# The four block sums of the second up projection: transfers that accumulate in place of VectorE

## The chip, the cores and the metric

The kernel runs on one core of a Trainium2 chip. The metric is the time of one execution in microseconds (us) on the device. Five engines take part, each with its own queue worked in order: TensorE (PE in the profile; its weight loads are PEld), VectorE (DVE), ScalarE (ACT), GpSimd (POOL) and SyncE (SP), which here issues all DMA transfers. Sixteen DMA engines carry them out.

## The reference

One layer of a block over 512 tokens of width 1024, in float32: an FFN half step, a mixer of two head groups, and a second FFN half step. The change is in the second FFN:

```python
def _modulate(x, shift, scale):
    return _rms(x) * (1.0 + scale[:, None, :]) + shift[:, None, :]

def _swiglu(h, w_in, w_out):
    gate, up = jnp.split(h @ w_in, 2, axis=-1)
    return (jax.nn.silu(gate) * up) @ w_out

h = _modulate(x, sh3, s3)
x = x + 0.5 * g3[:, None, :] * _swiglu(h, ffn2_w_in[l], ffn2_w_out[l])
```

`ffn2_w_in` is 1024 x 5632: 22 blocks of 128 gate columns and 22 blocks of 128 up columns. `h` has 512 rows.

## The kernel before

Activations lie transposed: 8 tiles of 128 channels x 512 tokens. To keep float32 accuracy every operand of a matmul is split into a high part (a cast to the matmul's type fp32r) and a low part (the rest), and a product is three matmuls: high x high, high x low, low x high. For weights, ScalarE casts the raw block (`wr`) to the high part (`wh`), and VectorE subtracts that from the raw block to get the low part (`wl`).

A **unit** is a block of weights: a load by SyncE into a raw tile of 128 x 1024 (pool tag `wr`, four buffers), and a split into `wh` and `wl` (four buffers each). `plan_units` lists all units in the order of use; `next_unit` takes the next, so loads are written just ahead of use, but SyncE runs ahead as far as raw buffers are free.

The second FFN's up projection (`ffn2`, line 936) computes blocks 0 to 4 and 18 to 21 as plain units. Blocks 5 to 17 (`SEVEN`), 13 of them, are done in pairs: gate block and up block together. `unit_pair` (line 227) loads both, and the gate block `g` and up block `u`, each cut into two halves of 512 input channels, form a 2 x 2 matrix of blocks: a11, a12 from `g` and a21, a22 from `u`. The 512 channels x 256 tokens quarters of the activations form the other 2 x 2 matrix. Their product is made of **seven** block products in place of eight. For that the weights are needed as a11, a12, a22 and as four sums: a21 + a22, that less a11, a11 - a21, and a12 less the second sum. The activations need four differences too, made once by `combined` (line 281) while blocks 2 to 4 run.

`sevenths` (line 234) prepares the weights of a pair in steps. VectorE makes the sums into two tiles of their own (`sf`, two buffers): the first two sums (lines 255 and, through the helper of line 240, `sub`), later the other two (line 240). Three wide splits follow, of `g`, of the first two sums and of the last two (ScalarE at line 244, VectorE at line 240), and a narrow one of a22 (ScalarE at line 274, tiles `sh`, `sl`).

`seven_products` (line 308) runs the seven products of a pair in the order 1, 2, 6, 7, 5, 4, 3, each 12 matmuls at line 323 into PSUM accumulators `za`, `zb`, `zc`. ScalarE and VectorE empty the accumulators between them (lines 327 to 343), since some are continued by later products; line 345 multiplies the SiLU of the gate half by the up half. After each product `side.step()` writes one step of the next pair's `sevenths`, so the weights of a pair are prepared while the pair before it is multiplied. What is left is flushed at the pair's end.

Within an engine the order of instructions is not simply that of the text: the framework's planner takes what has its inputs and buffers ready by its own cost figures, earlier text first. It also inserts all the waits. Some stages fix an order by hand (`in_order`, `matmuls_in_order`); the pairs are not among them.

Of the kernel before, what the change touches and what calls it, by code (L numbers as in the profile page):

```python
# [11 lines left out]
F32 = mybir.dt.float32  # L12
F32R = mybir.dt.float32r
# [3 lines left out]
ALU = mybir.AluOpType  # L17
AX = mybir.AxisListType

P = 128  # L20
# [4 lines left out]
DFF = 2816  # L25
# [16 lines left out]
class Side:  # L42
# [5 lines left out]
    def add(self, *gens):  # L48
        self.todo.extend(gens)
# [40 lines left out]
class Block:  # L90
# [136 lines left out]
    def unit_pair(self, w, c):  # L227

        raws = [self.raw_tile() for _ in range(2)]
        for raw, o in zip(raws, (c, DFF + c)):  # L230
            self.load(raw, w[:, o:o + P].rearrange("(k p) f -> p k f", p=P))
        return lambda: self.sevenths(*raws)

    def sevenths(self, g, u):

        nc = self.nc
        lo4, hi4 = slice(0, 4), slice(4, 8)
        a11, a12, a21, a22 = g[:, lo4], g[:, hi4], u[:, lo4], u[:, hi4]
        new = lambda dt, tag: self.seven.tile([P, 8, P], dt, tag=tag, name=self.name(tag))
        sub = lambda out, x, y: nc.vector.tensor_tensor(out=out, in0=x, in1=y, op=ALU.subtract)  # L240

        def parts(raw, n=8):
            hi, lo = (self.wp.tile([P, 8, P], F32R, tag=t, name=self.name(t)) for t in ("wh", "wl"))
            nc.scalar.copy(hi[:, :n], raw[:, :n])  # L244
            yield hi, lo
            sub(lo[:, :n], raw[:, :n], hi[:, :n].bitcast(F32))
            yield

        def steps():
            out = {}  # L250
            gate = parts(g)
            hi, lo = next(gate)
            out[1], out[2] = (hi[:, lo4], lo[:, lo4]), (hi[:, hi4], lo[:, hi4])
            s12, s34 = new(F32, "sf"), new(F32, "sf")
            nc.vector.tensor_tensor(out=s12[:, lo4], in0=a21, in1=a22, op=ALU.add)
            sub(s12[:, hi4], s12[:, lo4], a11)
            yield
            next(gate)
            p12 = parts(s12)
            hi, lo = next(p12)  # L260
            out[5], out[6] = (hi[:, lo4], lo[:, lo4]), (hi[:, hi4], lo[:, hi4])
            yield
            sub(s34[:, lo4], a11, a21)
            sub(s34[:, hi4], a12, s12[:, hi4])
            yield
            next(p12)
            p34 = parts(s34)
            hi, lo = next(p34)
            out[7], out[3] = (hi[:, lo4], lo[:, lo4]), (hi[:, hi4], lo[:, hi4])
            yield  # L270
            next(p34)
            yield
            hi, lo = (self.seven.tile([P, 4, P], F32R, tag=t, name=self.name(t)) for t in ("sh", "sl"))
            nc.scalar.copy(hi, a22)
            sub(lo, a22, hi.bitcast(F32))
            out[4] = hi, lo
            yield
            self.weights7 = out
        return steps()

    def combined(self):

        nc, v = self.nc, self.nc.vector
        f = lambda x: x.bitcast(F32)
        l, r = slice(0, HALF), slice(HALF, NT)
        sub = lambda out, x, y: v.tensor_tensor(out=out, in0=x, in1=y, op=ALU.subtract)
        self.t7 = {1: [], 2: [], 3: [], 4: []}
        for j in range(4):
            x = []
            for h in (self.h[j], self.h[j + 4]):  # L290
                x.append(self.slot(s="hx"))
                v.tensor_tensor(out=x[-1], in0=f(h[0]), in1=f(h[1]), op=ALU.add)
            yield
            a, b = x
            t12, t34 = self.slot(s="t7"), self.slot(s="t7")
            sub(t12[:, l], a[:, r], a[:, l])
            sub(t12[:, r], b[:, r], t12[:, l])
            yield
            sub(t34[:, l], b[:, r], a[:, r])
            sub(t34[:, r], b[:, l], t12[:, r])  # L300
            yield
            for t, n in ((t12, 1), (t34, 3)):
                hi, lo = self.split(t, "t")
                self.t7[n].append((hi[:, l], lo[:, l]))
                self.t7[n + 1].append((hi[:, r], lo[:, r]))
            yield

    def seven_products(self, w, side):

        nc = self.nc  # L310
        l, r = slice(0, HALF), slice(HALF, NT)
        half = lambda ks, ts: [(self.h[k][0][:, ts], self.h[k][1][:, ts]) for k in ks]
        xs = {1: half(range(4), l), 2: half(range(4, 8), l), 3: half(range(4, 8), r), 4: self.t7[4], 5: self.t7[1],
              6: self.t7[2], 7: self.t7[3]}
        za, zb, zc = self.acc()[:, :HALF], self.aux()[:, :HALF], self.aux()[:, :HALF]
        sa, sb, sg, up = (self.slot(s=n) for n in ("pa", "pb", "sg", "up"))

        def product(z, n, start):
            hi, lo = w[n]
            for j in range(4):  # L320
                xh, xl = xs[n][j]
                for i, (a, b) in enumerate(((hi, xh), (hi, xl), (lo, xh))):
                    nc.tensor.matmul(z, a[:, j, :], b, start=start and j == 0 and i == 0, stop=j == 3 and i == 2,  # L323
                                     skip_group_check=not start)
            side.step()

        add = lambda out, x, y: nc.vector.tensor_tensor(out=out, in0=x, in1=y, op=ALU.add)
        product(za, 1, True)
        nc.scalar.copy(sa[:, l], za)
        product(zc, 2, True)  # L330
        add(sg[:, l], zc, sa[:, l])
        nc.scalar.activation(sg[:, l], sg[:, l], AF.Silu)
        product(za, 6, False)
        nc.scalar.copy(sa[:, r], za)
        product(zb, 7, True)
        nc.scalar.copy(sb[:, l], zb)
        product(za, 5, False)
        nc.scalar.copy(sb[:, r], za)
        product(zb, 4, False)
        add(up[:, r], sb[:, l], sb[:, r])  # L340
        add(up[:, l], zb, sa[:, r])
        product(za, 3, False)
        nc.scalar.activation(sg[:, r], za, AF.Silu)
        a = self.slot(s="af")
        self.mul(a, sg, up)
        return a

    def unit_wide(self, src):
# [1736 lines left out]
```

## Time and profile before

| what | value |
|---|---|
| median of 2 runs | 1064.16 us (1063.7 to 1064.62) |
| profiled execution | 1067.01 us |
| its span, first to last instruction | 1065.3 us |
| mean granted clock of TensorE | 0.994 |
| TensorE busy | 1047.7 us, 98% of the span |
| VectorE busy | 649.5 us, 61% |
| ScalarE busy | 436.8 us, 41% |
| GpSimd busy | 24.9 us, 2% |
| bytes moved by DMA | 130.67 MB |

Times in a trace are counted from the first instruction. A line such as L240 is a line of the kernel; where a helper issues several operations they share its line and are told apart by their tiles (`out<-in`). A group's row gives the count, the total busy time and the mean of one, and then the idle time of the engine just before and what ended it. The releaser of a wait is inferred from the semaphores. The thirteen pairs run from about 760 to 893 us.

### The profile page before, as it was taken

To read this page: it belongs to the slowest core of one execution; us is meant where nothing else is said; L and a number is where in the kernel's file an instruction comes from. 1 tells how busy PE (TensorE), PEld (TensorE's weight loads), DVE (VectorE), ACT (ScalarE), POOL (GpSimd) and SP (SyncE) were. 2 spreads that over 40 slices of the span, in tenths; PEclk is the share of its full clock that TensorE was granted. 3 is DMA by queue.
4 is the path that set the end of the run, shared out by engine and by line. 5 is a ranking of instruction groups with operands and counts; after the bars stand their busy time and mean duration, and the time that the engine had idled before them with its cause. 6 is when DMAs were issued, how large, how long until landed. Compare 5 with 4: busy or idle time off the path is not lost.

```text
span 1065.3 us, 15289 instructions
## 1 busy us (share of the span) xinstructions
PE 1047.7 (98%) x6021; PEld 894.8 (84%) x6021; DVE 649.5 (61%) x1149; ACT 436.8 (41%) x772; POOL 24.9 (2%) x74
## 2 busy tenths in 40 slices
PE   6999999999999999999999989999999999999998
PEld 5788878788887799888788769998899999888887
DVE  4487984333576527557878567877878786532221
ACT  3342322222222215658865554444455555422220
POOL 1000000000000000100000001100000000000000
PEclk8999999999999999999999999999999999999999
DMA  9979973333597324421222021105233433333320
GB/s 276 281 231 302 284 233 98 99 99 94 169 305 248 113 80 141 113 60 40 60 75 70 21 79 41 40 14 146 60 110 94 114 107 112 90 94 109 108 66 30
DMA packets 207766, 130.67 MB, mean 123 GB/s; under 512 B 13633, under 2 KB 191822, under 8 KB 207694
## 3 DMA queue, kind: packets, MB, share of 16 engines
q1 hardware_dynamic: 207694, 129.69, 41.2%
q8 instruction: 47, 0.77, 0.3%
q14 instruction: 25, 0.20, 0.1%
HBM read 127.18 MB, written 2.49 MB: 122 GB/s over the span
## 4 chain that ended last, share of the span: by engine, by line
PE 93%; DVE 3%; issue 1%; DMA 1%; SPq 0%; POOL 0%; ACT 0%; POOLq 0%
PE pa L431 22%; PE pa L433 22%; PE pa L432 22%; PE pa L323 7%; PE pb L323 5%; PE pb L1818 1%; DMA ar<-in_w_ada 1%; PE pb L580 1%; PE pb L432 1%; PE pb L431 1%; PE pb L433 1%; PE pb L1798 1%; PE pb L1418 1%; PE pb L1370 1%; PE pb L1800 0%
## 5 line engine op out<-in xcount | busy, mean ns | idle before, releaser
L205 ACT CAST wh<-wr 128x1024 fp32r<-128x1024 f32 (+1 forms) x138 | 139.6, 1015 | 359.2 <-PE pa L432 272.9
L206 DVE TENSOR_TENSOR wl<-wr,wh 128x1024 fp32r<-128x1024 f32 (+1 forms) x138 | 162.4, 1179 | 173.2 <-ACT wh L205 167.7
L431 PE MATMUL pa<-hh,wh 128*128 128x512 f32 (+1 forms) x629 | 243.6, 387 | 0.0
L433 PE MATMUL pa<-hh,wl 128*128 128x512 f32 (+1 forms) x629 | 241.2, 383 | 0.0
L432 PE MATMUL pa<-hl,wh 128*128 128x512 f32 (+1 forms) x629 | 241.1, 383 | 0.0
L431 PE MATMUL pa<-ah,wh 128*128 128x512 f32 (+1 forms) x396 | 146.3, 370 | 0.0
L433 PE MATMUL pa<-ah,wl 128*128 128x512 f32 (+1 forms) x396 | 144.9, 366 | 0.0
L432 PE MATMUL pa<-al,wh 128*128 128x512 f32 (+1 forms) x396 | 144.8, 366 | 0.0
L431 PEld LDWEIGHTS pa<-hh,wh 128*128 128x128 f32 x629 | 118.3, 188 | 25.4 <-issue 2.9
L433 PEld LDWEIGHTS pa<-hh,wl 128*128 128x128 f32 x629 | 118.3, 188 | 22.9 <-DVE wl L206 0.4
L432 PEld LDWEIGHTS pa<-hl,wh 128*128 128x128 f32 x629 | 118.4, 188 | 21.1 <-DVE hl L617 0.2
L431 PEld LDWEIGHTS pa<-ah,wh 128*128 128x128 f32 x396 | 74.7, 189 | 13.5 <-ACT wh L205 1.7
L433 PEld LDWEIGHTS pa<-ah,wl 128*128 128x128 f32 x396 | 74.7, 189 | 12.2
L432 PEld LDWEIGHTS pa<-al,wh 128*128 128x128 f32 x396 | 74.7, 189 | 11.9
L748 DVE SCALAR_TENSOR_TENSOR aa<-ar,sc,aa 128x512 f32<-128x512 f32 x98 | 73.2, 750 | 11.4 <-DMA ar<-in_w_ada 10.3
L794 DVE TENSOR_TENSOR af<-sg,pa 128x512 f32<-128x512 f32 x27 | 18.5, 686 | 50.3 <-PE pa L433 50.3
L240 DVE TENSOR_TENSOR wl<-sf,wh 128x1024 fp32r<-128x1024 f32 x26 | 31.9, 1225 | 21.0 <-ACT wh L244 20.2
L860 DVE SCALAR_TENSOR_TENSOR xT<-pa,mod,xT 128x512 f32<-128x512 f32 (+1 forms) x18 | 12.4, 692 | 50.9 <-PE pa L433 50.9
L244 ACT CAST wh<-sf 128x1024 fp32r<-128x1024 f32 x26 | 27.2, 1048 | 30.1 <-PE pa L323 12.4
L800 ACT CAST ah<-af 128x512 fp32r<-128x512 f32 x44 | 25.9, 621 | 16.2 <-DVE af L794 16.2
L431 PE MATMUL pa<-mh,wh 128*128 128x256 f32 (+1 forms) x96 | 31.8, 333 | 0.0
L432 PE MATMUL pa<-ml,wh 128*128 128x256 f32 (+1 forms) x96 | 30.9, 322 | 0.3 <-DVE ml L1846 0.3
(434 smaller groups left out, 1811.6 us busy)
## 6 DMA issues: line engine op xcount, KB each, us to landing
wr<-in_ffn_w_in SPq DMA_DIRECT2D x79, 512.0 KB, 4.8
ar<-in_w_ada SPq DMA_DIRECT2D x48, 512.0 KB, 6.2
wr<-in_ffn_w_out SPq DMA_DIRECT2D x32, 512.0 KB, 4.1
ar<-in_w_ada SPq DMA_DIRECT2D x48, 256.0 KB, 5.0
wr<-in_w_in SPq DMA_DIRECT2D x21, 512.0 KB, 3.6
wr<-in_ffn_w_out SPq DMA_DIRECT2D x16, 384.0 KB, 4.4
wr<-in_w_out SPq DMA_DIRECT2D x8, 512.0 KB
wr<-in_ffn_w_in SPq DMA_DIRECT2D x8, 384.0 KB, 7.2
```

Source lines behind the costliest of these rows:

```text
L205: self.nc.scalar.copy(hi, raw)
L206: self.nc.vector.tensor_tensor(out=lo, in0=raw, in1=hi.bitcast(F32), op=ALU.subtract)
L240: sub = lambda out, x, y: nc.vector.tensor_tensor(out=out, in0=x, in1=y, op=ALU.subtract)
L244: nc.scalar.copy(hi[:, :n], raw[:, :n])
L323: nc.tensor.matmul(z, a[:, j, :], b, start=start and j == 0 and i == 0, stop=j == 3 and i == 2, skip_group_check=not start)
L431: mm(out, wh, xh, start=start, stop=False)
L432: mm(out, wh, xl, start=False, stop=False)
L433: mm(out, wl, xh, start=False, stop=stop)
L748: nc.vector.scalar_tensor_tensor(out=acc, in0=a, scalar=sc, in1=acc, op0=ALU.mult, op1=ALU.add)
L794: nc.vector.tensor_tensor(out=a, in0=s, in1=pu, op=ALU.mult)
L800: nc.scalar.copy(ah, a)
L860: nc.vector.scalar_tensor_tensor(out=self.xT[t][:, ts], in0=p[:, ts], scalar=gate[:, t:t + 1], in1=self.xT[t][:, ts], op0=ALU.mult, op1=AL ...
```

## The change

The pair's loads get a third one: a22 once more, into a tile `s2` of its own (two buffers). `sevenths` no longer has tiles `sf`. The four sums are made by DMA transfers that add to what is at their destination (`accum_op=ALU.add`), issued by GpSimd, and they overwrite the raw tiles:

- g low half += u low half (a11 + a21),
- u low half += u high half (a21 + a22),
- s2 += g low half (a22 + a11 + a21),
- g high half += s2 (a12 + a22 + a11 + a21).

A transfer of this kind can only add, so the signs differ from before: the up block counts as negated. The differences in `combined` change signs accordingly, by a `scalar_tensor_tensor` with a factor of -1 in half of them, and line 345 multiplies by -1.

Since `g` is overwritten, its split comes first, and all four transfers are written in the step after it. Then `u` (now a21 + a22, and a22) is split in one wide split, `s2` in the narrow one, and `g` a second time in the last wide split. So there are three wide splits and one narrow one, as before.

```diff
-        return lambda: self.sevenths(*raws)
+        s2 = self.seven.tile([P, 4, P], F32, tag="s2", name=self.name("s2"))
+        self.load(s2, w[4 * P:, DFF + c:DFF + c + P].rearrange("(k p) f -> p k f", p=P))
+        return lambda: self.sevenths(*raws, s2)
...
+        plus = lambda out, x: nc.gpsimd.dma_start(out=out, in_=x, accum_op=ALU.add)
+
+        def parts(raw):
+            n = raw.shape[1]
+            pool, tags = (self.wp, ("wh", "wl")) if n == 8 else (self.seven, ("sh", "sl"))
+            hi, lo = (pool.tile([P, n, P], F32R, tag=t, name=self.name(t)) for t in tags)
+            nc.scalar.copy(hi, raw)
             yield hi, lo
+            nc.vector.tensor_tensor(out=lo, in0=raw, in1=hi.bitcast(F32), op=ALU.subtract)
             yield
+
+        def both(p):
+            hi, lo = p
+            return [(hi[:, x], lo[:, x]) for x in (lo4, hi4)]
 
         def steps():
             out = {}
-            gate = parts(g)
-            hi, lo = next(gate)
-            out[1], out[2] = (hi[:, lo4], lo[:, lo4]), (hi[:, hi4], lo[:, hi4])
-            s12, s34 = new(F32, "sf"), new(F32, "sf")
-            nc.vector.tensor_tensor(out=s12[:, lo4], in0=a21, in1=a22, op=ALU.add)
-            sub(s12[:, hi4], s12[:, lo4], a11)
-            yield
-            next(gate)
-            p12 = parts(s12)
...
-            sub(s34[:, lo4], a11, a21)
-            sub(s34[:, hi4], a12, s12[:, hi4])
...
+            part = parts(g)
+            out[1], out[2] = both(next(part))
+            yield
+            next(part)
+            plus(g[:, lo4], u[:, lo4])
+            plus(u[:, lo4], u[:, hi4])
+            plus(s2, g[:, lo4])
+            plus(g[:, hi4], s2)
+            yield
+            part = parts(u)
+            out[5], out[4] = both(next(part))
+            yield
+            next(part)
+            yield
+            part = parts(s2)
+            out[6] = next(part)
+            next(part)
+            yield
+            part = parts(g)
+            out[7], out[3] = both(next(part))
+            yield
+            next(part)
             yield
             self.weights7 = out
...
+            less = lambda out, x, y: v.scalar_tensor_tensor(out=out, in0=x, scalar=-1.0, in1=y, op0=ALU.mult, op1=ALU.subtract)
-            sub(t12[:, l], a[:, r], a[:, l])
-            sub(t12[:, r], b[:, r], t12[:, l])
+            sub(t12[:, l], a[:, l], a[:, r])
+            less(t12[:, r], t12[:, l], b[:, r])
             yield
             sub(t34[:, l], b[:, r], a[:, r])
-            sub(t34[:, r], b[:, l], t12[:, r])
+            less(t34[:, r], t12[:, r], b[:, l])
...
-        self.mul(a, sg, up)
+        nc.vector.scalar_tensor_tensor(out=a, in0=sg, scalar=-1.0, in1=up, op0=ALU.mult, op1=ALU.mult)
```

More of the change, by code (lines that the diff above doesn't have):

```diff
@@ L231, in unit_pair, with sevenths @@
             self.load(raw, w[:, o:o + P].rearrange("(k p) f -> p k f", p=P))
-        return lambda: self.sevenths(*raws)
-    def sevenths(self, g, u):
+        s2 = self.seven.tile([P, 4, P], F32, tag="s2", name=self.name("s2"))
+        self.load(s2, w[4 * P:, DFF + c:DFF + c + P].rearrange("(k p) f -> p k f", p=P))
+        return lambda: self.sevenths(*raws, s2)
+    def sevenths(self, g, u, s2):
         nc = self.nc
         lo4, hi4 = slice(0, 4), slice(4, 8)
[L238 to L244, printed above, removed]
+        plus = lambda out, x: nc.gpsimd.dma_start(out=out, in_=x, accum_op=ALU.add)
[4 more added lines that the diff above has]
+            nc.scalar.copy(hi, raw)
@@ L245, in parts @@
             yield hi, lo
-            sub(lo[:, :n], raw[:, :n], hi[:, :n].bitcast(F32))
+            nc.vector.tensor_tensor(out=lo, in0=raw, in1=hi.bitcast(F32), op=ALU.subtract)
             yield
+        def both(p):
+            hi, lo = p
+            return [(hi[:, x], lo[:, x]) for x in (lo4, hi4)]
         def steps():
             out = {}
-            gate = parts(g)
-            hi, lo = next(gate)
-            out[1], out[2] = (hi[:, lo4], lo[:, lo4]), (hi[:, hi4], lo[:, hi4])
-            s12, s34 = new(F32, "sf"), new(F32, "sf")
@@ L255, in steps @@
-            nc.vector.tensor_tensor(out=s12[:, lo4], in0=a21, in1=a22, op=ALU.add)
-            sub(s12[:, hi4], s12[:, lo4], a11)
-            yield
-            next(gate)
-            p12 = parts(s12)
-            hi, lo = next(p12)
-            out[5], out[6] = (hi[:, lo4], lo[:, lo4]), (hi[:, hi4], lo[:, hi4])
+            part = parts(g)
+            out[1], out[2] = both(next(part))
+            yield
+            next(part)
+            plus(g[:, lo4], u[:, lo4])
+            plus(u[:, lo4], u[:, hi4])
@@ L262, in steps @@
+            plus(s2, g[:, lo4])
+            plus(g[:, hi4], s2)
             yield
-            sub(s34[:, lo4], a11, a21)
-            sub(s34[:, hi4], a12, s12[:, hi4])
+            part = parts(u)
+            out[5], out[4] = both(next(part))
             yield
[L266 to L269, printed above, removed]
+            next(part)
             yield
-            next(p34)
+            part = parts(s2)
@@ L272, in steps @@
+            out[6] = next(part)
+            next(part)
             yield
[L273 to L276, printed above, removed]
+            part = parts(g)
+            out[7], out[3] = both(next(part))
+            yield
+            next(part)
             yield
```

## The prediction

> **What bounds the kernel now.** I read the page first: engine shares, then the chain that ended last.
>
> ```profile
> span 1065.3 us, 15289 instructions
> PE 1047.7 (98%) x6021; PEld 894.8 (84%) x6021; DVE 649.5 (61%) x1149; ACT 436.8 (41%) x772; POOL 24.9 (2%) x74
> ...
> PE 93%; DVE 3%; issue 1%; DMA 1%; SPq 0%; POOL 0%; ACT 0%; POOLq 0%
> ```
>
> TensorE is busy 98% of the span and is 93% of the chain; VectorE is no bound of the whole. The change touches one stage, the 13 pairs of seven products, so that stage is read by itself: first as a window, then its chain in order of time (start, length, work).
>
> ```profile
> core 0: us, PE busy (x) PEld busy (x) DVE busy (x) ACT busy (x) POOL busy (x), PEclk, DMA share, GB/s
> 789.70:891.40 101.70, 101.70 (x836) 100.71 (x836) 79.36 (x114) 56.89 (x99) 0.00 (x0) 1.00 0.37 107
> ```
>
> ```profile
> 799.55 3.04 PE pa L323 x24
> 802.59 1.44 PE pb L323 x12
> ...
> 881.42 3.04 PE pa L323 x24
> ```
>
> TensorE is busy all 101.70 us at the full granted clock of 1.00. A piece of 24 matmuls is product 3 of one pair with product 1 of the next. From 799.55 to 881.42 lie eight pairs, so a pair takes 81.87 / 8 = **10.23 us**, a product of 12 matmuls 1.44 us. VectorE, at 79.36 of 101.70 us, has room. Nothing in this stage waits for the sums, so **taking them off VectorE gains nothing here**; the only question is whether the transfers fit into 10.23 us.
>
> How the weights of the next pair are made in that time is in ScalarE's and VectorE's timelines for one pair (start, length, idle before it and its releaser in brackets).
>
> ```profile
> 811.34 1.05 ACT L244 CAST wh<-wr 128x1024 fp32r<-128x1024 f32 x1 [1.01 <-PE pa L323]
> 812.30 0.38 ACT L343 ACTIVATE sg<-pa 128x256 f32<-128x256 f32 x1
> ...
> 814.22 1.05 ACT L244 CAST wh<-sf 128x1024 fp32r<-128x1024 f32 x1 [0.99 <-PE pb L323]
> ...
> 818.55 1.05 ACT L244 CAST wh<-sf 128x1024 fp32r<-128x1024 f32 x1 [1.00 <-PE pa L323]
> 819.51 0.37 ACT L338 COPY pb<-pa 128x256 f32<-128x256 f32 x1
> 819.94 0.62 ACT L274 CAST sh<-wr 128x512 fp32r<-128x512 f32 x1
> 821.58 1.05 ACT L244 CAST wh<-wr 128x1024 fp32r<-128x1024 f32 x1 [1.02 <-PE pa L323]
> ```
>
> ```profile
> 812.42 1.23 DVE L240 TENSOR_TENSOR wl<-wr,wh 128x1024 fp32r<-128x1024 f32 x1
> ...
> 816.57 0.69 DVE L255 TENSOR_TENSOR sf<-wr 128x512 f32<-128x512 f32 x1
> 817.29 0.69 DVE L240 TENSOR_TENSOR sf<-sf,wr 128x512 f32<-128x512 f32 x1
> 819.63 1.23 DVE L240 TENSOR_TENSOR wl<-sf,wh 128x1024 fp32r<-128x1024 f32 x1 [1.65 <-ACT wh L244]
> ...
> 821.44 0.68 DVE L240 TENSOR_TENSOR sf<-wr,wr 128x512 f32<-128x512 f32 x1
> ```
>
> The copy of the raw gate block (811.34, released by TensorE) starts as the old pair's last product ends, because a wh buffer comes free only then; 10.24 us later (821.58) the next pair's does the same. The other two wide copies wait for matmuls too, never for sums: those at 816.57 and 817.29 already belong to the pair after, made from raw blocks that arrived early. The sums thus have a whole pair of lead, because they are written beside the raw blocks.
>
> **The change, part by part.**
>
> *Removed:* four 128x512 operations of VectorE per pair, 4 x 0.69 = 2.8 us, 52 in all, some 36 us of busy time. On the path: 0, TensorE covers them.
>
> *Small edits:* line 345's product and half of the differences in combined() turn from TENSOR_TENSOR into SCALAR_TENSOR_TENSOR.
>
> ```profile
> L748 DVE SCALAR_TENSOR_TENSOR aa<-ar,sc,aa 128x512 f32<-128x512 f32 x98 | 73.2, 750 | 11.4 <-DMA ar<-in_w_ada 10.3
> L794 DVE TENSOR_TENSOR af<-sg,pa 128x512 f32<-128x512 f32 x27 | 18.5, 686 | 50.3 <-PE pa L433 50.3
> ```
>
> That is 0.75 against 0.69 us: 0.06 x 13 = 0.8 us on an engine that waits anyway; 0 on the path. Without that cover it would be 0.8 us.
>
> *Added load:* a third transfer per pair on SyncE's queue, 256 KB. It is worth nothing by itself while raw blocks come early; below it counts in a bound.
>
> *Moved:* the sums now overwrite the raw blocks. The first transfer (g low += u low) must wait until the gate block is split, that is for the copy (1.05) and the subtraction (1.23) after a wh buffer comes free. So **the lead of a whole pair is gone** and the sums start 2.28 us into the current pair. The second transfer (u low += u high) overwrites what the first reads, and the third (s2 += g low) reads what the first wrote: both wait for its landing. The fourth waits for the third. They are issued by GpSimd in this order, so the fourth also stands behind every wait before it; nothing else on GpSimd is due in the stage (its busy time in the window above is 0.00).
>
> *What a landing costs.* The trace has no transfer from GpSimd and no accumulating one. The nearest rows (KB each, median us from issue to landing; the last line is of the first 8 us alone):
>
> ```profile
> wr<-in_ffn_w_in SPq DMA_DIRECT2D x79, 512.0 KB, 4.8
> xt<-in_x SPq DMA_DIRECT2D x8, 256.0 KB, 3.1
> fr<-in_ffn_w_in SPq DMA_DIRECT2D x6, 256.0 KB, 3.9
> t_d<-bt SPq DMA_DIRECT2D x2, 64.0 KB, 2.0
> ```
>
> ```profile
> ar<-in_w_ada SPq DMA_DIRECT2D x2, 512.0 KB, 8.7
> ```
>
> Call the landing L. Ends: 2.0 us (64 KB, quiet) and 8.7 us (512 KB, all engines busy); no row allows less than nothing. I take **4.8 us**: an accumulating transfer of 256 KB must read 256 KB of source and 256 KB of destination, which is the 512 KB of the first row, and that row was taken in the same kind of surroundings, beside other weight loads.
>
> *The loop that this closes.* ScalarE takes its work in order. The copy of the summed u block needs two landings; the copy of s2 (0.62, as for sh above) comes behind it. In before, the next pair's gate copy stood behind all the copies of the pair ahead of it (818.55, 819.94, then 821.58); I assume that it still stands behind those two. Then from one gate copy to the next:
>
> 1.05 (copy) + 1.23 (subtraction) + 2 x 4.8 (landings) + 1.05 (u copy) + 0.62 (s2 copy) = **13.55 us**, against 10.23.
>
> The pair is bound by this loop, not by TensorE: 3.32 us more. It turns 12 times in the stage, since the first of the 13 pairs is prepared while ordinary units run. 12 x 3.32 = 39.8 us.
>
> Two other loops stay below it. The gate block is split a second time for products 7 and 3, which needs three landings: 2.28 + 14.4 + 2.28 = 18.96 us after its first copy. But product 7 of that pair starts only three products (4.3 us) into the pair, and a pair in which it is late lengthens the time for the next one: over two pairs 18.96 + 4 x 1.44 = 24.7, or 12.4 each. The raw buffers are held until then, and a new load follows, 4.8 and about 1 us for the third block: 24.8 per two pairs, 12.4 each. Both are near 13.55, so a longer L would not stay hidden in another place.
>
> *The clock.* TensorE would now pause in each pair. What pauses do here:
>
> ```profile
> 12.10:14.30 2.20, 0.06 (x1) 0.00 (x0) 2.20 (x7) 0.00 (x0) 1.02 (x1) 1.00 1.13 317
> 14.30:14.90 0.60, 0.23 (x5) 0.22 (x9) 0.60 (x4) 0.00 (x0) 0.00 (x0) 1.00 1.10 327
> 14.90:21.90 7.00, 6.72 (x35) 4.89 (x28) 4.20 (x10) 1.92 (x3) 1.14 (x32) 0.52 1.15 304
> ```
>
> After 2.2 idle us the granted clock was 0.52 for 7 us. In our loop TensorE isn't the bound: at half clock for 6.6 us of a pair it would use up the 3.3 us of pause and no more. I count 0; if it falls for longer, it costs up to 3 us a pair, part of the upper side.
>
> **Sum.** The profiled execution took 1067.0 us (span 1065.3 and 1.7 around it): 1067.0 + 39.8 = 1106.8. The median of the runs shown is 1064.2, 2.8 below it, so 1064.2 + 39.8 = **1104.0 us**. The forecast's own range, L from 4.1 to 5.5, gives loops of 12.15 to 14.95, that is 1087 to 1121.
>
> **Rivals.**
>
> *The transfers fit (not slower).* The loop is 3.95 + 2 L; it equals 10.23 at L = 3.14. The 3.1 of the row xt, the same 128 rows of 2 KB, is below that: 3.95 + 6.2 = 10.15, nothing lost, **1064**. For it: data that stay on the chip, and DMA engines with a mean share of only 0.37 in the window above. Against it: the destination is read as well, the weight loads of 1.25 MB fall into the same stretch as the first two transfers, and a semaphore round lies between issues. The Trainium skill speaks for this rival: "DMA: Bandwidth & Descriptors", section on the anatomy of one DMA on the gpsimd path, fits a transfer as about 2.0 us plus its bytes at 436 GB/s, an estimate of 2.6 us for 256 KB, by which the loop would be 9.2 us and the time 1064. That fit is for transfers in general, none said to accumulate, and no run of before shows one. Chance 0.25.
>
> *The second gate copy stands ahead of the next gate copy.* The order is the planner's, which goes by its own cost figures; if it takes the transfers for shorter than they are, the copy that needs three landings goes ahead of the next pair's first. Then the loop is 1.05 + 1.23 + 3 x 4.8 + 1.05 = 17.73 us, 7.50 more than now, 12 x 7.5 = 90: **1154**. For it: the fourth transfer would be done about when the pair ends, a near tie. Against it: in before, the first gate copy went ahead of the old pair's SiLU (811.34 before 812.30), so it is taken as soon as its buffer is free. In between lies a u copy ahead of the emptying of product 5 (819.51): 5.14 + 2 L = 14.74 us, 1118. Chance of this family 0.30.
>
> *A gain.* VectorE's freed 2.8 us a pair would have to shorten something that TensorE waits for; the window shows no idle TensorE. Chance of over 2% faster: 0.02.
>
> **How the numbers follow.** Forecast 0.43, fit 0.25, longer loop 0.30, gain 0.02. 2% of 1064 is 21 us, about what a measurement here can tell from no change; it is reached at a loop of 12.0 us, L = 4.0. Fit gives "same", with a small part of the forecast; so faster 0.02, same 0.28, slower 0.70. The range goes from the fit, 1061 with the spread of the runs, to 1160 just above the longer loop; left out are L above some 6 us in that loop and the clock's worst (8.7 us would give 21.35 and 1197 even in the forecast's loop).
>
> **What would show it.** Right: pairs of 13 to 14 us in the chain; ScalarE idle before the copy of u, released by a DMA; first-to-second transfer distance near 4.8 us; TensorE idle some 3 us a pair ahead of weights; VectorE's busy time down by about 35 us; nothing changed before 740 us or after the stage. Wrong: pairs of 10.23 us (the transfers fit), or a wait of ScalarE for the fourth transfer standing in front of the next gate copy (the longer loop). The forecast fails most easily by L, and next by the place of ScalarE's copies in its order.

## The result, and the profile after

The changed kernel takes **1149.4 us** (median) against 1064.2: a ratio of 1.0789, with a 95% interval of 1.0768 to 1.081. It is slower by 85 us; the forecast was 40 us slower. 1149.4 lies within the range that was given and within 5 us of the rival called "the second gate copy stands ahead of the next gate copy" (1154). The time of an experiment that is given without a ratio is that of one run.

The page of the kernel after: span, engine shares, and the chain that ended last.

```profile
span 1148.5 us, 15378 instructions
PE 1078.7 (94%) x6021; PEld 916.2 (80%) x6021; DVE 619.9 (54%) x1097; ACT 436.6 (38%) x772; POOL 70.7 (6%) x126
...
PE 74%; issue 15%; DMA 5%; DVE 3%; POOL 2%; SPq 0%; ACT 0%; POOLq 0%; ACTq 0%; DVEq 0%
```

VectorE's busy time is 29.6 us less. The forecast said about 35: the rows of the 52 sums do add up to some 36 us, but neighbouring operations overlap in the trace, and busy time counts an overlap once. TensorE has 31.0 us more busy time for the same 6021 matmuls. Its share of the chain fell from 93 to 74%; transfers rose from 1 to 5%, GpSimd from 0 to 2%. The windows put the difference behind 760 us, into the stage of the pairs: for the kernel after, the time up to 740 us, the step into the stage, the stage, and what comes behind it; then the stage before.

```profile
0.00:740.00 740.00, 725.03 (x4032) 603.49 (x4033) 471.02 (x905) 308.74 (x568) 24.94 (x74) 1.00 0.46 136
740.00:760.00 20.00, 20.00 (x98) 16.88 (x98) 11.11 (x18) 7.28 (x11) 3.69 (x4) 1.00 0.56 118
760.00:980.00 220.00, 169.18 (x1094) 157.32 (x1093) 83.87 (x114) 77.00 (x136) 42.03 (x48) 0.84 0.64 136
980.00:1148.50 168.50, 164.44 (x802) 138.53 (x800) 53.87 (x63) 43.56 (x60) 0.00 (x0) 1.00 0.30 86
```

```profile
760.00:893.10 133.10, 133.04 (x1084) 130.59 (x1083) 105.24 (x153) 73.00 (x128) 0.00 (x0) 1.00 0.35 100
```

In the stage TensorE is now busy for 169.18 of 220 us, at a mean granted clock of 0.84 in place of 1.00. The pair can be followed in GpSimd's timeline, where each transfer's issue stands with what the queue waited for.

```profile
850.29 0.87 POOL L240 DMA_DIRECT2D wr<-wr  x1 [7.17 <-DVE wl L248]
854.03 0.87 POOL L240 DMA_DIRECT2D wr<-wr  x1 [2.87 <-DMA wr<-wr]
854.58 1.22 POOL L240 DMA_DIRECT2D s<-wr  x1
859.15 0.87 POOL L240 DMA_DIRECT2D wr<-s  x1 [3.35 <-DMA s<-wr]
867.14 0.87 POOL L240 DMA_DIRECT2D wr<-wr  x1 [7.12 <-DVE wl L248]
```

From the first transfer of one pair (850.29) to that of the next (867.14) lie **16.85 us**; over eleven pairs, from 764.06 to 953.94, the mean is 17.3. The old pair was 10.23, and 12 x 7.0 = 84 us is the loss. ScalarE's timeline tells why the first transfer of a pair starts so late.

```profile
857.47 1.05 ACT L246 CAST wh<-wr 128x1024 fp32r<-128x1024 f32 x1 [0.83 <-DMA wr<-wr]
858.89 0.62 ACT L246 CAST sh<-s 128x512 fp32r<-128x512 f32 x1 [0.37 <-DMA s<-wr]
859.41 0.36 ACT L332 COPY pa<-pa 128x256 f32<-128x256 f32 x1
860.74 0.42 ACT L335 ACTIVATE sg<-sg 128x256 f32<-128x256 f32 x1 [0.97 <-DVE sg L330]
863.40 1.99 ACT L246 CAST wh<-wr 128x1024 fp32r<-128x1024 f32 x2 [2.24 <-DMA wr<-s]
```

The last line is two wide copies in one piece: the gate block's second copy, released by the fourth transfer, and directly behind it the **next pair's first gate copy**. So the loop has three landings in a row: first transfer 3.45 and 0.29 to the next issue, 0.87 for the second's issue, third 4.25 (counted from there), fourth 4.25, then 3.74 for two copies and the subtractions: 16.85. TensorE waits mainly at two places of the pair (the last column names who):

```profile
859.83 0.39 PE L326 MATMUL pa<-th,sh 128*128 128x256 f32 x1 [1.09 <-ACT pa L332]
864.50 0.39 PE L326 MATMUL pb<-th,wh 128*128 128x256 f32 x1 [2.61 <-ACT wh L246]
...
865.45 0.39 PE L326 MATMUL pa<-hh,wh 128*128 128x256 f32 x1 [0.45 <-ACT wh L246]
```

Product 6 waits for the emptying of product 1, which stands behind the copy of s2 in ScalarE's queue, and product 7 for the second gate copy: it starts as the first of the two copies in that piece ends. The third line, a matmul of the next pair (activations `hh`), waits 0.45 us more, for the other one. And the landings themselves, from 740 to 1000 us (KB each, median us; the transfers that add are those of POOLq):

```profile
q0 software_dynamic: 7488, 13.63, 33.7%
...
wr<-wr POOLq DMA_DIRECT2D x26, 256.0 KB, 3.5
s<-wr POOLq DMA_DIRECT2D x13, 256.0 KB, 4.3
wr<-s POOLq DMA_DIRECT2D x13, 256.0 KB, 4.2
```

### The profile page after: what moved, and what is told of

It reads as the page before. It is cut to its first block, busy times and chain, and to the rows that moved or that the text cites. A ratio compares the mean times of both kernels' runs of the same rounds, so it can differ in the third digit from the quotient of the medians.

```text
span 1148.5 us, 15378 instructions
## 1 busy us (share of the span) xinstructions
PE 1078.7 (94%) x6021; PEld 916.2 (80%) x6021; DVE 619.9 (54%) x1097; ACT 436.6 (38%) x772; POOL 70.7 (6%) x126
## 3 DMA queue, kind: packets, MB, share of 16 engines
q0 software_dynamic: 7488, 13.63, 7.6%
## 4 chain that ended last, share of the span: by engine, by line
PE 74%; issue 15%; DMA 5%; DVE 3%; POOL 2%; SPq 0%; ACT 0%; POOLq 0%; ACTq 0%; DVEq 0%
PE pa L434 20%; PE pa L435 20%; PE pa L436 20%; DMA wr<-wr 4%; POOL wr L240 1%; POOL s L240 1%; PE pb L1821 1%; PE pb L1801 1%; PE pb L434 1%; PE pb L435 1%; PE pb L436 1%; PE pb L583 1%; PE pb L1421 1%; DMA ar<-in_w_ada 1%; PE pb L1803 0%
## 5 line engine op out<-in xcount | busy, mean ns | idle before, releaser
L248 DVE TENSOR_TENSOR wl<-wr,wh 128x1024 fp32r<-128x1024 f32 x39 | 46.8, 1223 | 67.2 <-ACT wh L246 67.2
L326 PE MATMUL pb<-th,wh 128*128 128x256 f32 x104 | 37.0, 355 | 30.1 <-ACT wh L246 30.1
L246 ACT CAST wh<-wr 128x1024 fp32r<-128x1024 f32 x39 | 39.7, 1045 | 53.5 <-DMA wr<-s 31.5
L326 PEld LDWEIGHTS pb<-th,wh 128*128 128x128 f32 x104 | 25.6, 246 | 33.0 <-ACT wh L246 32.9
L191 POOL TENSOR_TENSOR ry<-ve,mhalf 128x4 f32<-128x4 f32 (+1 forms) x16 | 16.6, 1038 | 377.3 <-DVE ve L719 238.8
```

What stands on the lines that cost most here:

```text
L191: nc.gpsimd.tensor_tensor(out=y, in0=v, in1=self.mhalf[:, :n], op=ALU.pow)
L246: nc.scalar.copy(hi, raw)
L248: nc.vector.tensor_tensor(out=lo, in0=raw, in1=hi.bitcast(F32), op=ALU.subtract)
```

## The experiments

Theory A: a loop through ScalarE's queue with three landings sets the pair. Its rivals: summing in place (B), the load of the DMA engines (C), the number of buffers (D).

**VectorE makes the sums in place.** Everything of the change stays, the third load and the signs too; only the engine of the sums goes back.

```diff
-        plus = lambda out, x: nc.gpsimd.dma_start(out=out, in_=x, accum_op=ALU.add)
+        plus = lambda out, x: nc.vector.tensor_tensor(out=out, in0=out, in1=x, op=ALU.add)
```

> The four sums stay where the change has them (in place of the raw blocks, after the gate block's first split), but VectorE makes them: no transfer from GpSimd. Theory A (a loop through ScalarE's queue, from the second copy of the gate block to the next pair's first copy and through three landings one after another, sets the pair): without landings the loop is 1.05 + 1.23 for the first copy and its subtraction, three dependent sums of 0.69 and 1.05 for the second copy, some 5.5 us, under the 10.23 us of TensorE; pairs of 10.2 to 10.5 us and 1062 to 1070 us. Rival B (summing in place is itself what costs, since it takes away the lead of a pair): pairs stay well above 11 us, over 1075 us.

Measured: 1063.8 us, ratio 0.9986 (0.9975 to 0.9997). B falls: the overwriting, the third load and the sign edits together cost nothing that can be measured. All of the loss is in the transfers.

**One landing fewer in the chain.**

```diff
-            plus(g[:, hi4], s2)
+            plus(g[:, hi4], g[:, lo4])
```

> The fourth transfer adds the low half of the gate block in place of s2, so it needs one landing before it and not two; the same bytes move, and the weights of product 3 are other numbers. Theory A: the loop loses one landing of about 4.25 us and keeps the issue of two transfers more, so pairs of 13 to 14 us in place of 16.9, 1098 to 1115 us. Rival C (the DMA engines' load, a mean share of 0.65 in the stage, sets the pair): the bytes are the same, so 1140 to 1150 us.

Measured: 1118.2 us, 31 us less than the change with the same bytes. C alone falls. It is 3 us more than A's bound: the second, third and fourth transfers are now issued directly behind one another, and the fourth, which still ends the loop, lands in 5.2 us (median) in place of 4.2.

**Tiles of its own for the second gate split**, and **the same with the order tied back**. The first takes the second split out of the rotation of `wh` and `wl`. Both copies drew their tile from the same four buffers; in the builds where they share them and GpSimd moves the sums, the second gate copy stands just ahead of the next first copy in every pair.

```diff
-        def parts(raw):
+        def parts(raw, own=False):
...
+            pool, tags = (self.wp, ("wh", "wl")) if n == 8 and not own else (self.seven, ("gh", "gl") if own else ("sh", "sl"))
+            hi, lo = (pool.tile([P, n, P], F32R, tag=t, name=self.name(t), **({"bufs": 1} if own else {})) for t in tags)
...
-            part = parts(g)
+            part = parts(g, True)
             out[7], out[3] = both(next(part))
```

> The second split of the gate block gets tiles of its own (one buffer each) and no longer takes its turn in the four wh and wl buffers, so the next pair's first copy may stand ahead of it in ScalarE's queue, as the forecast had assumed. Everything else is the change's. Theory A: the loop then has two landings: 1.05 + 1.23 + 0.3 + 3.45 + 0.3 + 0.9 + 4.25 + 0.62 = 12.1 us to the end of the copy of s2, so pairs of 11.5 to 13 us and 1078 to 1098 us. Rival C (load of the DMA engines): the bytes are the same, so 1140 to 1150 us.

> As the run with tiles of its own for the second split, but the next pair's first copy is tied behind the second copy of the pair before, which gives ScalarE the order that it has in the change. Theory A: the order alone brings the loop with three landings back, pairs of about 17 us and 1143 to 1153 us. Rival D (the order does nothing, the number of buffers does): the time of the run with tiles of its own, under 1100 us.

Measured: 1108.9 us, ratio 1.0385 (1.0354 to 1.0416), with tiles of its own, and 1150.0 us with the order tied back. **The order alone is worth 41 us**; D falls. With the order tied back, ScalarE has the two copies where the change has them, told apart here by their tiles (`gh` is the second gate copy):

```profile
863.32 1.04 ACT L246 CAST gh<-wr 128x1024 fp32r<-128x1024 f32 x1 [2.36 <-DMA wr<-s]
864.27 1.04 ACT L246 CAST wh<-wr 128x1024 fp32r<-128x1024 f32 x1
```

Why the shared buffers give that order is not shown: that they are given out in the order of the text is a reading of this pair of runs, and no run kept the sharing and added buffers. With its own tiles the loop has the two landings that the forecast had drawn:

```profile
842.17 0.87 POOL L240 DMA_DIRECT2D wr<-wr  x1 [1.99 <-DVE wl L248]
846.40 0.87 POOL L240 DMA_DIRECT2D wr<-wr  x1 [3.37 <-DMA wr<-wr]
846.95 1.22 POOL L240 DMA_DIRECT2D s<-wr  x1
852.35 0.87 POOL L240 DMA_DIRECT2D wr<-s  x1 [4.17 <-DMA s<-wr]
855.21 0.87 POOL L240 DMA_DIRECT2D wr<-wr  x1 [1.99 <-DVE wl L248]
```

```profile
852.09 0.62 ACT L246 CAST sh<-s 128x512 fp32r<-128x512 f32 x1 [0.93 <-DMA s<-wr]
852.61 1.04 ACT L246 CAST wh<-wr 128x1024 fp32r<-128x1024 f32 x1
```

The next first copy (852.61) stands behind the copy of s2 and no longer behind the fourth transfer; the loop has two landings and takes 13.04 us here, and from 12.7 to 15.3 over the stage, 13.7 in the mean. My expectation of 1078 to 1098 was too low: the third transfer landed in 5.3 us (median) in place of 4.3, and two of the pairs' first transfers waited for a weight load. The mean share of the DMA engines was 0.81 here (770 to 930 us) and 0.65 in the change; that this is why landings grew is likely, but no run shows it apart.

```profile
s<-wr POOLq DMA_DIRECT2D x11, 256.0 KB, 5.3
wr<-s POOLq DMA_DIRECT2D x11, 256.0 KB, 5.5
```

**What a landing is made of.** Two runs on the change: the transfers as plain copies, and with a quarter of the bytes.

```diff
-        plus = lambda out, x: nc.gpsimd.dma_start(out=out, in_=x, accum_op=ALU.add)
+        plus = lambda out, x: nc.gpsimd.dma_start(out=out, in_=x)
```

> The four transfers of the change as plain copies without adding, with the same places and waits; the sums are left out, so the weights of five products are other numbers. The forecast priced a landing at 4.8 us because the destination is read too; the change showed 3.5, 4.3 and 4.2. If the adding is what makes them long, plain copies land in 2.6 to 3.1 us, the loop of 16.9 us loses 3 to 4 us and the time is 1100 to 1118 us. If a landing is mostly fixed cost, the time stays at 1130 to 1150 us.

```diff
-            plus(g[:, lo4], u[:, lo4])
-            plus(u[:, lo4], u[:, hi4])
+            plus(g[:, 0:1], u[:, 0:1])
+            plus(u[:, 0:1], u[:, 4:5])
...
```

> The four transfers of the change carry a quarter of the bytes each (one block of 128 columns in place of four, 64 KB), with the same waits; three quarters of the sums are left out. If a landing is mostly fixed cost, it stays at 2.0 to 2.6 us, the loop of three landings at 11 to 12.5 us and the time at 1074 to 1092 us. If it goes with the bytes, landings are near 1 us, the loop falls under TensorE's 10.23 us and the time is 1062 to 1068 us.

Measured: 1097.8 us as plain copies and 1097.6 us with a quarter of the bytes. The landings of the plain copies, and then of the quarters (770 to 910 us):

```profile
q0 software_dynamic: 3280, 10.75, 20.4%
...
wr<-wr POOLq DMA_DIRECT2D x21, 256.0 KB, 3.1
s<-wr POOLq DMA_DIRECT2D x10, 256.0 KB, 2.6
wr<-s POOLq DMA_DIRECT2D x10, 256.0 KB, 2.3
```

```profile
wr<-wr POOLq DMA_DIRECT2D x22, 64.0 KB, 2.6
wr<-s POOLq DMA_DIRECT2D x11, 64.0 KB, 2.4
s<-wr POOLq DMA_DIRECT2D x10, 64.0 KB, 2.7
```

The third and fourth transfers land in 2.3 to 2.6 us as copies and in 4.2 to 4.3 when they add: **adding costs 1.7 to 1.9 us per 256 KB** in that place. Most of what remains does not go with the bytes: 64 KB that add take 2.4 to 2.7, much like 256 KB that do not. (Copies of 64 KB were not run.) The plain run came out 2 us below what was said for "the adding makes them long", although its two wide copies start some 0.5 us after the fourth landing, behind the SiLU of line 335. The quarter run missed its 1074 to 1092 by 6 us: its landings are near the 2.0 to 2.6 that were expected, but the first of a pair still took up to 4.1 us, beside the weight loads.

**The lead given back.** If the loop through ScalarE is all, transfers issued a pair earlier should be hidden. `head` writes a pair's first gate split and its four transfers.

```diff
-        raws = [self.raw_tile() for _ in range(2)]
+        raws = [self.raw_tile(), self.seven.tile([P, 8, P], F32, tag="ru", name=self.name("ru"), bufs=3)]
...
+            now = late
+            if f + 2 in SEVEN:
+                late = self.next_unit(ahead=0)
+                side.add(head(late))
             if f + 1 in SEVEN:
-                side.add(self.next_unit(ahead=0))
+                side.add(now)
```

> The change's transfers with their lead given back: the second split of the gate block has tiles of its own, the up blocks have three raw buffers of their own, and the gate block's first split and the four transfers of a pair are written one pair earlier, ahead of the splits of the sums of the pair before. No copy on ScalarE then stands directly behind a transfer that has just been issued. Theory A (landings in ScalarE's loop cost the time): all landings are hidden, pairs of 10.1 to 10.4 us, 1061 to 1070 us. Rival C (the DMA engines are the next bound: share 0.81 of 13.6 us, some 11.0 us of packets a pair): pairs of 11 us or more, 1072 to 1080 us.

Measured: 1105.5 us, ratio 1.0389 (1.0372 to 1.0406). Both theories missed. GpSimd's timeline shows a loop that was not in either:

```profile
821.29 0.87 POOL L240 DMA_DIRECT2D wr<-s  x1 [5.67 <-DMA s<-wr]
821.84 1.22 POOL L240 DMA_DIRECT2D wr<-ru  x1
828.92 0.87 POOL L240 DMA_DIRECT2D ru<-ru  x1 [5.86 <-DMA wr<-ru]
829.47 1.22 POOL L240 DMA_DIRECT2D s<-wr  x1
834.95 0.87 POOL L240 DMA_DIRECT2D wr<-s  x1 [4.26 <-DMA s<-wr]
```

The next pair's first transfer (821.84) is ready and goes out together with the old pair's fourth, so data and ScalarE no longer hold it back. But GpSimd's queue is in order: it waits for the first transfer's landing, then for the third's, and only then comes the next pair. Two landings in a row, from 821.29 to 834.95, are 13.66 us. The DMA engines are also as busy as in the run with tiles of its own; the last columns of a window are the granted clock, their mean share and GB/s:

```profile
800.00:850.00 50.00, 38.08 (x291) 36.71 (x290) 23.17 (x29) 20.34 (x36) 12.32 (x14) 0.91 0.82 173
```

The queue became theory E, and two runs tested it: the same kernel with a quarter of the bytes, and with plain copies.

> The run with the lead given back, with transfers of a quarter of the bytes (64 KB, the rest of the sums left out). In the full-size run GpSimd's queue itself was the loop: it waits for the first transfer of a pair (6.3 us, issued together with the fourth of the pair before) and then for the third (5.2 us), 12.5 to 13 us a pair with the issues. Theory E (GpSimd's queue, two landings in a row per pair): with landings of 2.4 to 2.7 us two of them and their issues take 7 us, less than TensorE's 10.23, so nothing is lost: 1061 to 1068 us. Rival F (what was lost there came from the split's order and buffers): 1090 to 1107 us as before.

> The run with the lead given back, with the four transfers as plain copies of full size (no adding; the sums are left out). Theory E: landings of 2.3 to 3.5 us, two in a row and their issues 7 to 8.5 us, under 10.23: 1061 to 1070 us. Then the adding is what makes the transfers too long even with the lead. Rival F: 1090 to 1107 us.

Measured: 1065.5 and 1067.5 us, beside 1065.8 for the kernel before. F falls: with the same order and buffers, shorter or lighter transfers lose next to nothing. The windows of the two show TensorE busy again:

```profile
770.00:880.00 110.00, 109.75 (x900) 108.20 (x899) 66.16 (x87) 61.90 (x110) 36.18 (x41) 1.00 0.64 143
```

```profile
770.00:880.00 110.00, 108.22 (x885) 106.55 (x884) 65.55 (x86) 61.21 (x108) 21.74 (x40) 1.00 0.70 211
```

The times are E's, but its landings are not. With a quarter of the bytes the first transfer lands in 2.7 us in place of 6.3, while the third still takes 5.3, as at full size (5.2):

```profile
s<-wr POOLq DMA_DIRECT2D x10, 64.0 KB, 5.3
```

So in most pairs two landings and their issues took nearly 10 us, not 7, and E's loop only just fits under TensorE's 10.23. Both runs also lower the DMA engines' share, from 0.82 to 0.64 and 0.70. That the queue adds the two landings up is read in the trace; how much of their length is that load was not separated.

**VectorE in place, in more rounds.**

> The sums in place by VectorE once more, in more rounds, since it read 0.9986 of before: its pairs take 7 x 1.44 = 10.08 us in place of 10.23, the pause at the boundary between pairs being gone. 13 x 0.15 = 2.0 us, so a ratio of 0.997 to 0.999; if that was the spread of the runs, 1.000.

Measured: 0.9985 (0.9974 to 0.9996). It is the fastest version seen, by 0.15%, too little to matter. In the first profile of this same kernel the chain in order of time shows pairs of 7 x 1.44 = 10.08 us: the two pieces of 24 matmuls here take 2.88 us, 3.04 in before.

```profile
827.84 2.88 PE pa L326 x24
...
837.92 2.88 PE pa L326 x24
```

## Why the prediction was wrong

- **The bound, and the sums at no cost: right.** TensorE bound the stage. With the sums off VectorE and the transfers hidden (the quarter-size run with the lead), TensorE was busy 109.75 of 110 us and the time was 1065.5 against 1065.8: nothing gained. VectorE making the sums costs nothing either (0.9986).
- **The small edits and the third load at 0: right**, by the run with VectorE in place.
- **The lead lost, and a loop in place of TensorE as the bound: right.** The stage went from 10.23 to some 17 us a pair, and up to 760 us nothing changed.
- **The step that failed** is the place of the next first gate copy: "I assume that it still stands behind those two", the copies of the u block and of s2. It stands behind the second gate copy too, so three landings were in the loop and not two: 17.3 us a pair in place of 13.55. The row that the assumption cites had shown it: in before, the next gate copy (821.58) stands behind all three wide copies, the one at 818.55 among them. There each waited only for TensorE to free a buffer, so that the order cost nothing. The rival with three landings had been priced at 1154 with a chance of 0.30. The reason given against it was that a first copy is taken as soon as its buffer is free; in the change it was not taken ahead of the second gate copy in any pair.
- **The number of the assumed order: near, in part by luck.** With the second split in tiles of its own that order came about and took 1108.9 us, 5 us from the forecast of 1104.0; tied back it took 1150.0. But in the pair shown the copy of u lies beside the third landing and not in the loop, where the forecast counts 1.05 us for it; the gaps and issues that are in the loop (0.29 and 0.55) were not counted; and the two landings came to some 9.1 us against 9.6.
- **The landing: mis-sized.** 4.8 us was taken; 3.5, 4.3 and 4.2 were measured, with 0.29 to the next issue and 0.87 for the issue between. In the three-landing loop that came to 16.85 against 17.73. The reason given, that the destination is read too, fits the plain copies (2.3 to 3.1) but was not shown apart from other costs of adding.
- **"The transfers fit": wrong, and not by the adding alone.** The rival counts two landings of 3.14 us at most, 6.28 together. As plain copies the first transfer of a pair landed in some 3.3 us and the third in 2.6, which fits, and their run still took 1097.8 us: the second gate copy, which waits for the fourth, still stood ahead of the next first copy. The estimate of 2.6 us from the fit on the page "DMA: Bandwidth & Descriptors" of the Trainium skill (its section on the anatomy of one DMA) agrees with these plain copies, 2.3 to 3.1; the transfers that add took 3.5 to 4.3, and plain copies in the run with the lead 3.0 to 5.0.
- **The clock at 0: not tested alone.** TensorE did slow down: the clock was 0.84 over the stage, and 0.50 from 850.3 to 852 us, behind a wait of 2.47 us. The chain of the loop from 850.29 to 867.14 contains no matmul, so the slower clock lies in its shadow there. And the run with plain copies lost 33 us at a clock of 0.99 in the stage (766 to 920 us).

What stays open: whether GpSimd's queue, written so that it waits once and not twice per pair, would hide the transfers, or whether the DMA engines' load would then be the bound. A share of 0.82 of the 13.66 us above is already some 11 us a pair, more than TensorE's 10.23. It was not tried.

## What to carry to other kernels

Work taken off an engine that isn't the bound gains nothing, and it can cost when it comes back as latency: four dependent transfers have three landings, and no transfer of GpSimd here, copy or sum, 64 or 256 KB, landed in less than 2.2 us. Look at which in-order queue stands behind each landing: here ScalarE's with three, and once that was mended GpSimd's own with two. When two uses share a rotation of buffers, look whether one that is ready stands behind one that is late: here it did, and tiles of its own for the late one were worth 41 us.

## What the runs showed of the hardware that was not expected

- A transfer that adds occupies the DMA engines much longer than a copy of the same bytes: 33.7% of 260 us for 13.63 MB against 20.4% of 140 us for 10.75 MB, that is 6.4 against 2.7 us of all sixteen engines per MB.
- Its issue on GpSimd shows as 0.87 us, that of a plain copy in the same place as 0.55 us.
- With four of them a pair, landings grew as the pairs got shorter: the third from 4.3 us (pairs of 17, the DMA engines' share 0.65) to 5.3 (pairs of 13.7 in the mean, share 0.81).
- The bytes did not set a landing alone: 64 KB that add landed in 2.7 us in one kernel and in 5.3 us in the same place of another, with shorter pairs.
